# The first feed-forward product by seven products of half the token width, with its weight sums on GpSimd

## The chip, the core and the metric

The kernel runs on one core of a Trainium2 chip. The metric is the device time of one execution in microseconds (us); lower is better. The engines of a core are called as the profile calls them: PE is TensorE (PEld its weight loads), DVE is VectorE, ACT is ScalarE, POOL is GpSimd and SP is SyncE, which only issues transfers here. SBUF is the on-chip memory that all of them read, PSUM holds the sums that PE makes (POOL does not use it here), HBM is the chip's main memory.

## What is computed

An encoder of two layers on 512 tokens of width 1024, all in 32-bit floats. Each layer adds to x the result of two attention groups, and then that of a feed-forward part, with a norm ahead of each; a last norm ends the network. Only the feed-forward part is changed:

```python
h = rmsnorm(x, mlp_norm[l])
u = jnp.square(jax.nn.relu(jnp.einsum('bsd,df->bsf', h, w_ff1[l])))   # 1024 -> 4096: the first product
x = x + jnp.einsum('bsf,fd->bsd', u, w_ff2[l])                        # 4096 -> 1024: the second product
```

## The kernel before, in words

**Numbers in two parts.** PE multiplies a rounded 32-bit format. So that little is lost, each operand is split in two: hi, the rounded value, and lo, the remainder. A product is three matmuls, hi by hi, hi by lo and lo by hi; `three` (L284) issues them. A weight tile is split by two instructions, a copy that rounds on ACT (`round`, L109) and a subtraction raw - hi on DVE (L125). Activations are split the same way by `split` (L232 to L235).

**Weights.** `_unit_list` (L50) writes down all weight units in the order in which PE uses them. `_Weights` loads raw units of 128 x 1024 by SP's queue into a ring of three tiles (`load`, L98), splits them (`do_split`, L132) and hands them out (`next`, L153). While a unit is being used, units up to three behind it may be split: `next` asks for four from the one in use, and there are four places for split tiles in the feed-forward part. Hooks kept in `W.then` start what may follow the split of a unit (L150).

**The feed-forward part** (from L826) works in 4 groups of 1024 of the 4096 inner columns (`GROUPS`, L25). A group has two stages:

- *The first product*, L1012: eight blocks of 128 inner columns. `block` (L297) runs 8 x 3 matmuls with 512 tokens as the moving operand, from a unit of kind "1". `evict_u` (L873) takes the result out of PSUM: relu and square on ACT, and then the seven forms of u that the second product needs, by subtractions on DVE (L889, L892), each split in hi and lo.
- *The second product*, L1022: a product of 2 x 2 by 2 x 2 blocks by the seven-product algorithm (in Winograd's form), so seven block products in place of eight. Their names are in `FORMS` (L41). Each form has two weight units of kind "f" of 12 matmuls of 512 columns each. The sums of weight quarters that the forms need are made by the transfers: a tile is loaded by SP's queue, and another quarter is added in flight by an accumulating transfer that POOL issues (`grow` and `fetch`, L842 to L857). `gather` (L901) adds finished chains to the result y on DVE, with the norm's factor.

Each group's second product follows its first at once; PE works through both in the order of the program. PSUM has 8 banks in four sets: "mm" 2, "s" 3, "o" 1 and "t" 2 (L170). Instructions are queued on each engine in an order that the framework fixes at compile time from the program's order and its own estimates; `behind` adds an order by hand. A queue is worked off in that order: an instruction that waits holds up those behind it.

**x, cos and sin.** x stays in SBUF through the feed-forward part and gets y added at the end of layer 0 (`back`, L923). The cos and sin tables are loaded again for layer 1 in group 1 of layer 0. In layer 1 the same two tiles take the gains of the last norm (L1006), which `weigh` and `store` (L968 to L981) use at the very end. The attention part comes ahead of each feed-forward part; its softmax-like weights are multiplied on POOL (`s1_sb`, L539) and its norm on POOL too (`finish`, L686).

Of the kernel before, what the change touches and what calls it, by code (L numbers as in the profile page):

```python
# [41 lines left out]
SIDE = {"11": 0, "x4": 1, "21": 2, "x3": 3, "x1": 4, "x2": 5, "22": 6}  # L42
HOME = {"11": 0, "x1": 0, "x3": 1, "x2": 1, "x4": 1, "22": 2, "21": 2}
CHAIN = {"11": "X", "x2": "X", "x1": "X", "22": "X", "x3": "V", "x4": "V", "21": "Y"}
# [5 lines left out]
def _unit_list():  # L50
# [5 lines left out]
    for l in range(L):  # L56
# [13 lines left out]
        for g in range(GROUPS):  # L70
            for f in range(2 * GP):
                units.append(("1", l, g * 2 * GP + f))
            for form in FORMS:
                for c in range(GP // 2):
                    units.append(("f", l, g, form, c))
# [6 lines left out]
_RING = [i for i, u in enumerate(_UNITS) if u[0] != "f"]  # L82
_SLOT = {u: n for n, u in enumerate(_RING)}
_QUAD = [(l, g, q, c) for l in range(L) for g in range(GROUPS) for c in range(GP // 2) for q in QUADS]


class _Weights:
    def __init__(self, nc, dram, rawp, splp):
        self.nc, self.dram, self.rawp = nc, dram, rawp
        self.loaded = self.split = self.used = self.turn = 0  # L90
        self.raw, self.tiles, self.home, self.then = {}, {}, {}, {}
        self.depth = 3
        self.eager = False
        self.pools = [splp]
        self.owner = {}
        self.rest_of = {}

    def load(self, n):  # L98
        while self.loaded < min(n, len(_RING)):
# [28 lines left out]
    def spot(self, i):  # L128
        n = 2 * len(self.pools) if _UNITS[i][0] in "1f" else 2
        return self.turn % n if self.turn < n else 0  # L130

    def do_split(self, n, ahead=None):  # L132
        while self.split < min(n, len(_UNITS)):
# [4 lines left out]
            if kind != "f":  # L138
                self.load(_SLOT[i] + 1)
# [8 lines left out]
            if kind != "f":  # L148
# [14 lines left out]
def trunk(ctx, tc, opened, xT, w, w2, gfin, lamv, cos, sin, out):  # L163
# [4 lines left out]
    ps = ctx.enter_context(tc.tile_pool(name="ps", bufs=2, space=PSUM))  # L168

# [18 lines left out]
    ssq = cp.tile([P, S], F32, tag="ssq", name="ssq")  # L188
    rbc = cp.tile([P, S], F32, tag="rbc", name="rbc")
    cos_t = cp.tile([P, S], F32, tag="cos", name="cos_t")  # L190
    sin_t = cp.tile([P, S], F32, tag="sin", name="sin_t")
# [40 lines left out]
    def split(hi, lo, src):  # L232
        a = nc.scalar.activation(hi, src, AF.Copy)  # L233
        nc.vector.tensor_tensor(out=lo, in0=src, in1=hi.bitcast(F32), op=ALU.subtract)  # L234
        return a  # L235
# [87 lines left out]
    for l in range(L):  # L323
# [502 lines left out]
        with ExitStack() as fctx:  # L826
# [9 lines left out]
            kept = [[fp.tile([P, 1024], F32, tag=f"q{k}{c}", name=f"q{k}{c}_{l}0") for c in range(GP // 2)] for k in range(3)]  # L836
            i0 = W.used

            def unit(g, form, c):
                return i0 + g * (2 * GP + len(FORMS) * GP // 2) + 2 * GP + FORMS.index(form) * GP // 2 + c  # L840

            def fetch(g, form, c):  # L842
                k = HOME[form]
                if g:
                    kept[k][c] = fp.tile([P, 1024], F32, tag=f"q{k}{c}", name=f"q{k}{c}_{l}{g}")
                W.raw[unit(g, form, c)] = kept[k][c]
                nc.sync.dma_start(kept[k][c], quad(g, "12" if form == "x3" else form, c))
                if form == "x3":
                    nc.gpsimd.dma_start(kept[k][c], quad(g, "22", c), accum_op=ALU.add)

            def grow(g, form, q, c):
                t = kept[HOME[form]][c]
# [4 lines left out]
                W.raw[unit(g, form, c)] = t  # L857

            for g in range(GROUPS):
                for c in range(GP // 2):  # L860
                    for form, fn, args in (
                            ("11", grow, (g, "x1", "12", c)), ("x3", grow, (g, "x2", "11", c)),
                            ("x2", grow, (g, "x4", "21", c)), ("21", grow, (g, "22", "22", c)),
                            ("x1", fetch, (g + 1, "11", c)), ("x4", fetch, (g + 1, "x3", c)),
                            ("22", fetch, (g + 1, "21", c))):
                        if g + 1 < GROUPS or fn is grow:
                            W.then.setdefault(unit(g, form, c), []).append(lambda fn=fn, args=args: fn(*args))
            for form in ("11", "x3", "21"):
                for c in range(GP // 2):
                    fetch(0, form, c)  # L870
            W.pools.append(f2)

            def evict_u(pt, g, k, forms):  # L873
                pair, which = k // 2, k % 2
                nm = f"{l}{g}{pair}"
                if which == 0:
                    forms[pair] = (
                        fp.tile([P, 8, 256], F32, tag="F", name="F" + nm),
                        fp.tile([P, 7, 256], F32R, tag="Ah", name="Ah" + nm, bufs=GP),
                        fp.tile([P, 7, 256], F32R, tag="Al", name="Al" + nm, bufs=GP))  # L880
                F, hi, lo = forms[pair]
# [3 lines left out]
                if which == 0:  # L885
# [3 lines left out]
                nc.vector.tensor_tensor(  # L889
                    out=F[:, 4:6, :], in0=F[:, 1:3, :], in1=F[:, 0:1, :].to_broadcast([P, 2, 256]), op=ALU.subtract)  # L890
                for o, i, j in ((6, 5, 1), (7, 6, 3)):
                    nc.vector.scalar_tensor_tensor(  # L892
                        out=F[:, o, :], in0=F[:, i, :], scalar=-1.0, in1=F[:, j, :], op0=ALU.mult, op1=ALU.subtract)
                W.forms = split(hi[:, 3:7, :], lo[:, 3:7, :], F[:, 4:8, :])
# [264 lines left out]
```

## Time and profile before

| | |
|---|---|
| median of 3 runs | 1146.6 us (1146.29 to 1146.64) |
| profiled execution | 1146.63 us, of it the span of the trace 1144.7 us |
| granted PE clock | 0.998 |
| instructions | 15843 |
| HBM read, written | 138.18 MB, 2.10 MB |

The profile's page gives for each engine its busy time, its share of the span and its number of instructions. Slices are the span in 40 equal parts, a digit being the busy share in tenths. A row of a group of instructions reads: line, engine, operation, output <- inputs, shapes, xcount | busy us in total, mean ns of one | idle time of the engine just before them, and what ended it. A row of the timeline reads: start (us from the start of the span), duration, engine, line, operation, and in brackets how long the engine had been idle and what released it. A row of the windows gives for one stretch of time its length and for each engine its busy time and number of instructions, then the granted clock, the share of the DMA engines and the rate of transfers. The recorded durations of successive matmuls overlap, as one starts before the last is through.

### The profile page before, as it was taken

How to read it: one execution, taken by the hardware profiler on the slowest of the kernel's cores; microseconds unless marked ns; L12 is line 12 of the kernel's file. 1: busy time of each engine (PE TensorE's matmuls, PEld its weight loads, DVE VectorE, ACT ScalarE, POOL GpSimd, SP SyncE). 2: the span in 40 equal slices, each digit the busy share in tenths (PEclk: the TensorE clock that was granted, in tenths of full speed). 3: DMA queues.
4: the chain of work that ended last, by engine and by line, in shares of the span. 5: the costliest groups of instructions: out<-in, count | busy, mean ns of one | idle time of the engine just before them, and what ended most of it. 6: DMA issues, size and time to landing. Idle time of an engine off the chain costs nothing.

```text
span 1144.7 us, 15843 instructions
## 1 busy us (share of the span) xinstructions
PE 1135.8 (99%) x5749; PEld 967.2 (84%) x5749; DVE 811.4 (71%) x1313; ACT 641.1 (56%) x1147; POOL 141.0 (12%) x225
## 2 busy tenths in 40 slices
PE   9999999999999999999999999999999999999997
PEld 7899889888888888888888998988888888888886
DVE  7898788775645756756778877887657467566576
ACT  6456666556656445455345666665574454553554
POOL 1000333100101101001000013330011011010010
PEclk9999999999999999999999999999999999999999
DMA  7664353257754845836226634522758458358162
GB/s 256 164 187 141 106 167 98 70 205 166 186 176 90 206 154 94 247 119 103 82 74 192 195 111 144 151 72 76 234 115 211 157 92 232 136 93 256 41 126 92
DMA packets 55853, 166.47 MB, mean 145 GB/s; under 512 B 6880, under 2 KB 8160, under 8 KB 55776
## 3 DMA queue, kind: packets, MB, share of 16 engines
q1 hardware_dynamic: 46128, 131.36, 35.3%
q0 software_dynamic: 9216, 33.56, 17.1%
q8 instruction: 45, 0.74, 0.3%
q10 hardware_dynamic: 432, 0.56, 0.1%
q14 instruction: 32, 0.26, 0.1%
HBM read 138.18 MB, written 2.10 MB: 123 GB/s over the span
## 4 chain that ended last, share of the span: by engine, by line
PE 98%; DVE 1%; issue 1%; ACT 0%; POOL 0%; POOLq 0%; DVEq 0%; ACTq 0%
PE f L287 10%; PE f L288 10%; PE f L289 10%; PE X L288 5%; PE X L287 5%; PE X L289 5%; PE wo L287 3%; PE wo L289 3%; PE wo L288 3%; PE V L288 2%; PE V L289 2%; PE V L287 2%; PE Y L289 1%; PE Y L287 1%; PE Y L288 1%; PE T1s L606 1%
## 5 line engine op out<-in xcount | busy, mean ns | idle before, releaser
L125 DVE TENSOR_TENSOR wlo<-raw,whi 128x1024 fp32r<-128x1024 f32 (+1 forms) x130 | 154.3, 1190 | 109.2 <-ACT whi L109 107.1
L109 ACT ACTIVATE whi<-raw 128x1024 fp32r<-128x1024 f32 (+1 forms) x130 | 131.8, 1018 | 142.3 <-PE f L288 44.5
L287 PE MATMUL f<-h_hi,whi 128*128 128x512 f32 x512 | 199.9, 390 | 0.0
L289 PE MATMUL f<-h_hi,wlo 128*128 128x512 f32 x512 | 199.6, 390 | 0.0
L109 ACT ACTIVATE whi<-q 128x512 fp32r<-128x512 f32 x224 | 129.9, 623 | 124.3 <-PE X L289 44.0
L288 PE MATMUL f<-h_lo,whi 128*128 128x512 f32 x512 | 199.5, 390 | 0.0
L125 DVE TENSOR_TENSOR wlo<-q,whi 128x512 fp32r<-128x512 f32 x224 | 145.5, 688 | 73.5 <-ACT whi L109 69.6
L289 PEld LDWEIGHTS f<-h_hi,wlo 128*128 128x128 f32 x512 | 96.2, 188 | 19.9
L287 PEld LDWEIGHTS f<-h_hi,whi 128*128 128x128 f32 x512 | 96.2, 188 | 19.7
L288 PEld LDWEIGHTS f<-h_lo,whi 128*128 128x128 f32 x512 | 96.2, 188 | 19.7
L234 DVE TENSOR_TENSOR Al<-F,Ah 128x256 fp32r<-128x256 f32 (+2 forms) x96 | 74.8, 779 | 46.0 <-ACT Ah L233 46.0
L287 PE MATMUL X<-whi,Ah 128*128 128x512 f32 x248 | 97.0, 391 | 0.0
L289 PE MATMUL X<-whi,Al 128*128 128x512 f32 x248 | 96.7, 390 | 0.0
L288 PE MATMUL X<-wlo,Ah 128*128 128x512 f32 x248 | 96.6, 390 | 0.0
L233 ACT ACTIVATE Ah<-F 128x256 fp32r<-128x256 f32 (+2 forms) x96 | 67.6, 704 | 50.0 <-DVE F L892 48.1
L856 POOL DMA_DIRECT2D q<-in_w x48 | 41.8, 871 | 424.0 <-DVE wlo L125 396.1
L289 PEld LDWEIGHTS X<-whi,Al 128*128 128x128 f32 x248 | 46.6, 188 | 9.7
L287 PEld LDWEIGHTS X<-whi,Ah 128*128 128x128 f32 x248 | 46.6, 188 | 9.5
L288 PEld LDWEIGHTS X<-wlo,Ah 128*128 128x128 f32 x248 | 46.6, 188 | 9.5
L287 PE MATMUL V<-whi,Ah 128*128 128x512 f32 x128 | 49.9, 390 | 0.0
L289 PE MATMUL V<-whi,Al 128*128 128x512 f32 x128 | 49.9, 390 | 0.0
L288 PE MATMUL V<-wlo,Ah 128*128 128x512 f32 x128 | 49.9, 390 | 0.0
(658 smaller groups left out, 2562.2 us busy)
## 6 DMA issues: line engine op xcount, KB each, us to landing
raw<-in_w SPq DMA_DIRECT2D x126, 512.0 KB, 3.5
q<-in_w SPq DMA_DIRECT2D x64, 512.0 KB, 5.5
q<-in_w POOLq DMA_DIRECT2D x64, 512.0 KB, 5.5
x<-in_xT SPq DMA_DIRECT2D x8, 256.0 KB, 4.4
out_xT<-y SPq DMA_DIRECT2D x6, 256.0 KB, 2.1
raw<-in_w SPq DMA_DIRECT2D x6, 128.0 KB, 4.1
cos_t<-in_cos SPq DMA_DIRECT2D x2, 256.0 KB, 4.9
sin_t<-in_sin SPq DMA_DIRECT2D x2, 256.0 KB, 4.0
```

The lines of the kernel that those rows point to most:

```text
L109: return self.nc.scalar.activation(o, src, AF.Copy)
L125: self.last = h, nc.vector.tensor_tensor(out=lo[:, a:b], in0=raw[:, a:b], in1=hi[:, a:b].bitcast(F32), op=ALU.subtract)
L233: a = nc.scalar.activation(hi, src, AF.Copy)
L234: nc.vector.tensor_tensor(out=lo, in0=src, in1=hi.bitcast(F32), op=ALU.subtract)
L287: nc.tensor.matmul(pt, ah, bh, start=first, stop=False, skip_group_check=goes_on)
L288: nc.tensor.matmul(pt, ah, bl, start=False, stop=False, skip_group_check=goes_on)
L289: nc.tensor.matmul(pt, al, bh, start=False, stop=last, skip_group_check=goes_on)
L606: nc.tensor.transpose(pt[:, off : off + P], u["w"][qi][:, kb * P : (kb + 1) * P], ident)
L856: nc.gpsimd.dma_start(t, quad(g, q, c), accum_op=ALU.add)
```

## The change

The first product of seven of the eight half groups of a layer is computed by the seven-product algorithm as well. The half (g, j) = (0, 0) stays as it was, four whole blocks. Each other half, a "quad group", covers 512 inner columns: seven forms, each with one unit of kind "s" of 128 x 1024 (two pairs of 128 columns by four pieces of the inner width 512), used by 2 x 4 x 3 matmuls with 256 tokens as the moving operand.

- **Forms of h.** During the four whole blocks `h_form` makes three forms of h from x with the norm's gain (16 DVE operations of 128x256, and splits), and overwrites a quarter of h with a fourth one.
- **Weight sums.** Four quarters of w_ff1 (roles a, b, c, d) are loaded for each quad group by SP's queue into five tiles: the three of the raw ring, the pair cos/sin and the pair ssq/rbc. Four sums of 128x1024 on POOL make the forms: e = c + b, b + a, a + e, d + a. Each is issued by a hook behind a split of the unit whose tile it overwrites or reads.
- **Evictions.** In a quad group three results are copied from PSUM by ACT, two are added and one is subtracted by DVE, and four differences and sums of 128x512 that make the forms of u run on POOL (`pool_tt`), in place of the subtractions on DVE. The whole blocks use POOL for theirs too, eight of 128x256.
- **x in HBM.** x's tile is the work space of the quad groups. In layer 0 eight stores on SP's queue put x into HBM at the start of the feed-forward part, and eight loads bring it back in the last group's second product. In layer 1, x has been turned into y before.
- **Tables.** cos and sin are loaded behind the last split of layer 0; the final gains are loaded into x's tile in the last group of layer 1.
- **Ring.** Raw units of the next layer are loaded only when the last quad group has been split (`limit`). The order of two forms in `SIDE` is exchanged.

The core of the diff:

```diff
+CHAIN1 = {"11": "X", "x3": "V", "x2": "X", "21": "Y", "x1": "X", "x4": "V", "22": "X"}
...
         for g in range(GROUPS):
-            for f in range(2 * GP):
-                units.append(("1", l, g * 2 * GP + f))
+            for j in range(2):
+                if (g, j) == (0, 0):
+                    units.extend(("1", l, f) for f in range(GP))
+                else:
+                    units.extend(("s", l, g, j, form) for form in FORMS)
...
+            def add(n, to, by, other=None):
+                if n < len(groups):
+                    nc.gpsimd.tensor_tensor(
+                        out=piece(n, to), in0=piece(n, other or to), in1=piece(n, by), op=ALU.add)
+
+            def first_sums(n):
+                add(n, "e", "c", "b")
+                add(n, "b", "a")
...
+            for n, (g, j) in enumerate(groups):
+                then(("s", l, g, j, "11"), add, n, "a", "e")
+                then(("s", l, g, j, "x3"), bring, n + 1, "c")
+                then(("s", l, g, j, "21"), add, n, "d", "a")
+                then(("s", l, g, j, "21"), bring, n + 1, "a")
+                then(("s", l, g, j, "x1"), bring, n + 1, "b")
...
+                then(("s", l, g, j, "22"), first_sums, n + 1)
...
+            if not last:
+                park = dp.tile([KC, P, S], F32, tag="park", name="park")
+                for c in range(KC):
+                    nc.sync.dma_start(park[c], x[:, c, :])
...
+            def scaled(out, c0, half, other, op):
+                for c in range(4):
                     nc.vector.scalar_tensor_tensor(
+                        out=out[:, c, :], in0=x[:, c0 + c, half], scalar=gcol("mlp", l, c0 + c), in1=other[:, c, :],
+                        op0=ALU.mult, op1=op)
...
+            def quad_group(g, j):
+                X, V = bank("mm", f"X{l}{g}{j}"), bank("s", f"V{l}{g}{j}")
+                Y = bank("o" if j else "s", f"Y{l}{g}{j}")
...
+                for n, form in enumerate(FORMS):
+                    u = W.next("s")
...
+                    for pr in range(2):
+                        for c in range(4):
+                            at = 512 * pr + P * c
+                            three(to[ch][:, 256 * pr : 256 * pr + 256], (u[0][:, at : at + P], u[1][:, at : at + P]),
+                                  (h[0][:, c, :], h[1][:, c, :]),
+                                  form in ("11", "x3", "21") and pr == c == 0, pr == 1 and c == 3, True)
+                    if form == "11":
+                        nc.scalar.copy(m11, X)
+                    elif form == "x3":
+                        nc.scalar.copy(v3, V)
+                    elif form == "x2":
+                        nc.scalar.copy(sx, X)
+                    elif form == "21":
+                        nc.vector.tensor_tensor(out=F[1], in0=Y, in1=m11, op=ALU.add)
+                        nc.scalar.activation(F[1], F[1], AF.Relu)
+                        nc.scalar.activation(F[1], F[1], AF.Square)
+                        split(hi[0], lo[0], F[1])
+                    elif form == "x1":
+                        nc.vector.scalar_tensor_tensor(
+                            out=F[2], in0=X, scalar=-1.0, in1=v3, op0=ALU.mult, op1=ALU.subtract)
+                    elif form == "x4":
+                        nc.vector.tensor_tensor(out=F[0], in0=V, in1=sx, op=ALU.add)
+                        nc.scalar.activation(both, both, AF.Relu)
+                        nc.scalar.activation(both, both, AF.Square)
+                        split(hi[1], lo[1], F[2])
+                        pool_tt(F[1], F[1], F[0], ALU.subtract)
+                        pool_tt(F[0], F[2], F[0], ALU.subtract)
+                        pool_tt(F[2], F[2], F[1], ALU.add)
...
+                        split_less(hi[5], lo[5], F[2])
+                    else:
+                        nc.scalar.activation(F[3], X, AF.Relu, scale=-1.0)
+                        nc.scalar.activation(F[3], F[3], AF.Square)
+                        split(hi[2], lo[2], F[3])
+                        pool_tt(F[3], F[2], F[3], ALU.subtract)
+                        W.forms = split(hi[6], lo[6], F[3])
```

243 lines of the change are left out of this document (167 added, 76 removed).

## The prediction, made before the changed kernel ran

> **What bounds the kernel now.** I read the page first: busy shares, the slices, the chain that ended last.
>
> ```profile
> PE 1135.8 (99%) x5749; PEld 967.2 (84%) x5749; DVE 811.4 (71%) x1313; ACT 641.1 (56%) x1147; POOL 141.0 (12%) x225
> ...
> PEclk9999999999999999999999999999999999999999
> ...
> PE 98%; DVE 1%; issue 1%; ACT 0%; POOL 0%; POOLq 0%; DVEq 0%; ACTq 0%
> ```
>
> PE does not idle, its clock is full, and 98% of the chain is PE. A gain can come only from fewer or shorter matmuls, and it lasts as long as what feeds PE keeps up. So the next view is the busy time by stage, here for one group of layer 0: first product, then second.
>
> ```profile
> core 0: us, PE busy (x) PEld busy (x) DVE busy (x) ACT busy (x) POOL busy (x), PEclk, DMA share, GB/s
> 323.00:366.00 43.00, 43.00 (x192) 35.63 (x191) 21.27 (x30) 23.80 (x37) 2.62 (x3) 1.00 0.40 104
> ...
> 447.00:485.00 38.00, 38.00 (x170) 31.48 (x169) 28.47 (x42) 18.35 (x29) 4.40 (x5) 1.00 0.80 198
> ```
>
> In the first product DVE is busy 21 of 43 us, in the second 28.5 of 38, and POOL almost never. The change puts work on both.
>
> **What PE gains.** A matmul's recorded length overlaps the next, so the price is the distance between starts. Two rounds of weights that each wait for a block of 24 matmuls of 512 columns, and a run of 256-wide matmuls:
>
> ```profile
> 333.30 1.06 ACT L109 ACTIVATE whi<-raw 128x1024 fp32r<-128x1024 f32 x1 [2.78 <-PE f L288]
> ...
> 344.18 1.06 ACT L109 ACTIVATE whi<-raw 128x1024 fp32r<-128x1024 f32 x1 [2.32 <-PE f L288]
> ```
>
> ```profile
> 583.69 0.28 PE L428 MATMUL p1w<-mdl,h_hi 128*128 128x256 f32 x1
> ...
> 586.09 0.28 PE L428 MATMUL p1w<-mdl,h_hi 128*128 128x256 f32 x1
> ```
>
> The first pair is two blocks apart: 10.88 us, 5.44 a block, 226.7 ns a matmul. The second is 20 matmuls apart: 2.40 us, 120 ns each. Per layer, 28 of the 32 blocks become 7 quad groups. Four blocks are 96 matmuls of 512, 21.76 us; a quad group is 7 forms of 24 matmuls of 256, 168 x 120 ns = 20.16 us. PE saves 1.60 us a quad group, 14 x 1.60 = **22.4 us** in all: half-width matmuls cost more than half, so of the eighth of the arithmetic little is left.
>
> The Trainium skill speaks for more: "TensorE: Matmul & The Clock Gate", "Back-to-back issue gap", gives a warm gap of N/2.4 plus 2.5 ns, 215.8 and 109.2 ns here. By that a quad group would save 20.7 - 18.3 = 2.4 us and the kernel 33 us. The rows, 226.7 and 120, disagree with it and decide.
>
> **What the other engines get.** Rows by form, and the second product's DMA issues on POOL:
>
> ```profile
> L125 DVE TENSOR_TENSOR wlo<-raw,whi 128x1024 fp32r<-128x1024 f32 x122 | 151.3, 1242 | 109.2 <-ACT whi L109 107.1 <-DMA q<-in_w 1.5 <-ACT lam_ex L315 0.3
> ...
> L109 ACT ACTIVATE whi<-raw 128x1024 fp32r<-128x1024 f32 x122 | 128.9, 1059 | 142.3 <-PE f L288 44.5 <-DMA raw<-in_w 24.5 <-PE V L289 20.9
> ...
> L856 POOL DMA_DIRECT2D q<-in_w x48 | 41.8, 871 | 424.0 <-DVE wlo L125 396.1 <-DMA q<-in_w 27.9
> L909 DVE SCALAR_TENSOR_TENSOR y<-X,r,y 128x512 f32<-128x512 f32 x58 | 41.7, 749 | 4.9 <-PE X L289 3.8
> L884 ACT ACTIVATE F<-F 128x512 f32<-128x512 f32 x64 | 40.3, 630 | 1.4
> L234 DVE TENSOR_TENSOR Al<-F,Ah 128x1024 fp32r<-128x1024 f32 x32 | 39.2, 1224 | 28.1 <-ACT Ah L233 28.1
> L883 ACT ACTIVATE F<-f 128x512 f32<-128x512 f32 x64 | 37.5, 587 | 12.9 <-DVE Al L234 8.0 <-PE f L289 4.9
> ...
> L892 DVE SCALAR_TENSOR_TENSOR F<-F 128x256 f32<-128x256 f32 x64 | 27.0, 422 | 1.1
> ...
> L889 DVE TENSOR_TENSOR F<-F 128x512 f32<-128x512 f32 x32 | 22.1, 689 | 6.5 <-ACT F L884 6.5
> ```
>
> *ACT, per quad group*: 7 weight rounds x 1.06 = 7.4; three copies out of PSUM x 0.59 = 1.8; relu, square and rounds at 0.63 for 512, 1.06 for 1024: F1 1.9, F0 with F2 4.4, F3 2.5. Together **18.0 us** in 20.2. It fits, without room.
>
> *DVE, per quad group*: 7 weight remainders x 1.24 = 8.7; one 1024-wide remainder 1.22; four of 512 at 0.69 and one scalar_tensor_tensor at 0.75 = 3.5; three operations that read PSUM, two at 0.69 and one at 0.75 = 2.1. **15.5 us**. The four blocks that it replaces cost 10.6 (half of 21.27): seven weight units stand where four stood.
>
> *POOL, per quad group*: four sums of 128x1024 and four of 128x512. No row shows a 1024-wide sum. The nearest are these; the first is by itself:
>
> ```profile
> 149.28 1.29 POOL L686 TENSOR_TENSOR os<-os,rb 128x512 f32<-128x512 f32 x1
> ```
>
> ```profile
> 143.05 1.09 POOL L539 TENSOR_TENSOR sig0s<-sig0s,C0s 128x512 f32<-128x512 f32 x1 [0.67 <-DVE C0s L536]
> ```
>
> ```profile
> 148.53 0.63 POOL L539 TENSOR_TENSOR sig0s<-sig0s,C0s 128x256 f32<-128x256 f32 x1 [1.63 <-DVE C0s L536]
> ```
>
> From 256 to 512 L539 grows by 0.46, so 1024 would take 1.09 + 0.92 = 2.0 us; scaled by L686, 1.29 x 2.0/1.09 = 2.37. I take 1.29 and 2.37, as the new sums read whole aligned tiles like os and rb: 4 x 2.37 + 4 x 1.29 = **14.6 us** (low end 12.4).
>
> **The point that decides: DVE and POOL get in each other's way.**
>
> ```profile
> 143.50 1.73 DVE L125 TENSOR_TENSOR wlo<-raw,whi 128x1024 fp32r<-128x1024 f32 x1
> ```
>
> ```profile
> 148.69 0.56 DVE L234 TENSOR_TENSOR xl<-T0s,xh 128x384 fp32r<-128x384 f32 x1 [0.31 <-ACT xh L233]
> ```
>
> ```profile
> 118.94 1.23 DVE L125 TENSOR_TENSOR wlo<-raw,whi 128x1024 fp32r<-128x1024 f32 x1 [0.38 <-ACT whi L109]
> ```
>
> ```profile
> 119.82 1.50 POOL L686 TENSOR_TENSOR os<-os,rb 128x512 f32<-128x512 f32 x1 [1.33 <-ACT rb L282]
> ```
>
> The remainder that starts at 143.50 falls into the POOL product of 143.05 to 144.14 and takes 1.73 us instead of 1.24: it waited until about 0.15 us before POOL's end. The other way round, the POOL product of 119.82 met a remainder that ran to 120.17 and took 1.50 instead of 1.29. At 148.69 a DVE operation with one operand in PSUM ran beside the POOL product of 148.53 in 0.56 us, unharmed. So a DVE operation with both operands in SBUF and a POOL product take turns. All remainders of weights are of that sort, 13.4 of DVE's 15.5 us, and so are all POOL sums.
>
> The Trainium skill states this as an exclusive lock ("SBUF — State Buffer", "Who interferes with whom"): the loser waits for the whole instruction. The trace agrees, to 0.15 us. By that rule alone, with nothing else late, each sum would block DVE for its whole length.
>
> **The sum.** I add DVE and POOL as one resource over a group, since the second product's 38 us let a backlog drain. Before, a group takes PE 8 x 5.44 + 14 x 2.72 = 81.6 us. After, PE needs 2 x 20.16 + 38.1 = 78.4. DVE and POOL need 28.5 (second product, row above) + 2 x 15.5 + 2 x 14.6 = **88.7 us**. So the pair is the bound, 7.1 us over the old time. Two corrections, that DVE's PSUM readers and the ends of a POOL sum can overlap, and that the chain round, remainder, sum, round leaves gaps, have opposite signs; I leave both out.
>
> The first group of a layer has one quad group. Its four whole blocks carry on DVE 5.0 of weights (4 x 1.24), 5.3 of evictions (two pairs, each 0.42 + 0.69 + 0.69 + 0.42 + 0.42), and the forms of h: 16 operations of 256 at 0.42 = 6.7 and four remainders at 1.24 = 5.0. That is 22.0 + 15.5 + 28.5 = 66.0 on DVE; POOL has 14.6 and eight differences of 256 x 0.63 = 5.0. Sum 85.6, 4.0 over.
>
> Six full groups and two first ones: 6 x 7.1 + 2 x 4.0 = **50.6 us longer**.
>
> *Moved at no cost, and their cover:* x goes to HBM in 8 stores (layer 0 only) and comes back in 8 loads on SP's queue; behind the stores stand the first loads of weight pieces. At the 198 GB/s of the quoted window 2.1 MB takes 10.6 us, covered by the units already split (four, 21.8 us); without cover, up to 10 us once. The loads run during the last second product, 38 us. The added waits on POOL: a sum waits for a weight remainder, and behind it in POOL's queue stand the second product's accumulating DMAs (0.87 us each), whose data the following weight rounds await. The final gains load later, in the last group, under its forms; by this row, up to 5 us if uncovered.
>
> ```profile
> cos_t<-in_cos SPq DMA_DIRECT2D x2, 256.0 KB, 4.9
> ```
>
> The profiled execution lasted 1146.6 us with a span of 1144.7, its 1.9 us outside kept; it is the median of the runs too. 1146.6 + 50.6 = **1197 us**.
>
> **Rivals.**
>
> *A. Everything hides*: PE stays the bound, 1146.6 - 22.4 = 1124 us. For it: ACT's 18.0 and DVE's 15.5 each fit in 20.2, and four units are split ahead. Against it: 15.5 + 14.6 = 30.1. It needs POOL to work beside DVE's PSUM readers and idle time only. Price per group at most -3.2 us; it decides from where DVE and POOL overlap by over 10.3 us a group (88.7 to 78.4). With 7.1 of them they break even. This is the faster side. 0.17.
>
> *B. Half overlaps*: with the low POOL price (12.4) and 0.3 us of each of the 16 sums free, a group needs 28.5 + 31 + 24.8 - 4.8 = 79.5, beside 81.6 before; gaps between waits bring it near the old time or above: 1140 to 1170. 0.20, a little of it faster or within the bound.
>
> *C. The backlog does not drain in the second product*, since splits run only four units ahead and POOL's queue is in order: each quad group takes its own 30.1 instead of 21.8. 14 x 8.3 = 116, 1263 us. For it: the sums for x3, x2, x4 form a chain round, remainder, sum. Against it: the second product's DVE has 9.6 us of room. 0.13.
>
> *D. The edit does not do what it says*: the 256-wide matmuls run slower than 120 ns because stationary weights change with every one. Each of the 5749 matmuls has its weight load in the quoted profile too, those of the run among them, so 0.02; at 130 ns it adds 14 x 1.68 = 24 us to PE alone.
>
> Forecast (1170 to 1235): 0.48.
>
> **How the numbers follow.** The range takes in B, and C's lower half: 1138 to 1250, which leaves out most of A and the top of C. Changes under 0.2%, 2.3 us, are about what a measurement of this kernel cannot tell from none. Faster: A and a little of B, 0.18. Within: 0.04. Slower: 0.78.
>
> **What would show it.** Right: in first-product windows PE busy falls below nine tenths; the remainders of weights (L125's group) have a mean over 1.24 us, 1.5 or more; POOL sums of 1024 show 2.0 us or more; the chain has DVE and POOL shares of several per cent. Wrong: PE stays at 99%, with L125 at 1.24. C is told from the forecast by second-product windows that stay at 38 us while every quad group takes 28 or more; D by start distances over 120 ns with no idle time before.

## The result, and the profile after

The changed kernel takes **1239.5 us** (median of 4 runs, 1237.6 to 1240.1); the kernel before takes 1146.6 us on the same chip. The ratio is 1.081, with a 95% interval of 1.079 to 1.083: **92.9 us longer**. The forecast was 1197, in a range up to 1250. So the sign and the mechanism have to be looked at apart from the size.

The page of the changed kernel: busy shares, granted clock, and the chain that ended last.

```profile
PE 1157.1 (93%) x6757; PEld 1017.6 (82%) x6757; DVE 973.4 (79%) x1349; ACT 706.4 (57%) x1227; POOL 408.9 (33%) x353
...
PEclk9999999989998998999999999999899999999999
...
PE 56%; DVE 18%; POOL 8%; issue 6%; ACT 6%; DMA 6%; POOLq 0%; DVEq 0%; SPq 0%; ACTq 0%
```

PE was 98% of the chain and is 56%. DVE and POOL together hold 26%, though DVE is busy only 79% of the span: no engine is full, and yet PE waits. The clock has dips that the kernel before didn't have.

The windows of a full group of layer 1: its two quad groups, then its second product.

```profile
958.20:1008.10 49.90, 44.23 (x337) 43.42 (x336) 40.26 (x32) 28.72 (x40) 27.46 (x13) 0.93 0.32 91
1008.10:1049.60 41.50, 39.62 (x171) 31.37 (x170) 31.89 (x44) 20.68 (x33) 13.76 (x11) 1.00 0.82 196
```

The group takes 91.4 us and took 81.6. A quad group takes 25.0 where four blocks took 21.8, and the second product 41.5 where it took 38.1. In the first row DVE and POOL add up to 67.7 us in 49.9: part of the recorded time of each is waiting for the other. The first groups of the two layers went from 82.1 to 101.4 and from 85.7 to 103.9 us, by the starts of their matmuls.

Groups of instructions, by form:

```profile
L951 POOL TENSOR_TENSOR x<-x 128x512 f32<-128x512 f32 x56 | 93.0, 1661 | 58.1 <-DVE Al L243 30.1 <-ACT x L1035 23.7 <-PE V L304 2.5
...
L132 DVE TENSOR_TENSOR wlo<-T,whi 128x1024 fp32r<-128x1024 f32 x56 | 93.1, 1663 | 34.8 <-ACT whi L116 34.7
...
L243 DVE TENSOR_TENSOR Al<-x,Ah 128x512 fp32r<-128x512 f32 x56 | 67.2, 1201 | 29.1 <-ACT Ah L242 29.1
...
L890 POOL TENSOR_TENSOR T<-T,T 128x1024 f32<-128x1024 f32 x20 | 55.1, 2755 | 15.9 <-DVE wlo L132 14.9
...
L1033 DVE TENSOR_TENSOR x<-V,x 128x512 f32<-128x512 f32 x14 | 9.5, 681 | 0.0
```

Weight remainders of the tiles T take 1663 ns, where the kernel before had 1242, and the remainders of u (L243) 1201 in place of 689, while L1033, which has one operand in PSUM, stayed at 681. The single instructions show how. The timeline of DVE:

```profile
962.22 2.10 DVE L132 TENSOR_TENSOR wlo<-T,whi 128x1024 fp32r<-128x1024 f32 x1 [1.53 <-ACT whi L116]
...
969.88 0.69 DVE L1025 TENSOR_TENSOR x<-Y,x 128x512 f32<-128x512 f32 x1 [0.69 <-PE Y L304]
...
972.71 2.88 DVE L243 TENSOR_TENSOR Al<-x,Ah 128x512 fp32r<-128x512 f32 x1
```

And the timeline of POOL over the same time:

```profile
960.82 2.41 POOL L890 TENSOR_TENSOR waves<-waves,T 128x1024 f32<-128x1024 f32 x1 [5.81 <-DVE wlo L132]
...
969.28 2.41 POOL L890 TENSOR_TENSOR norms<-T,T 128x1024 f32<-128x1024 f32 x1 [6.04 <-DVE wlo L132]
971.76 3.27 POOL L890 TENSOR_TENSOR T<-T,T 128x1024 f32<-128x1024 f32 x1
```

The remainder of 962.22 starts inside the sum of 960.82, which ends at 963.23, and ends 1.09 us after it: a whole remainder after the sum. The remainder of 512 at 972.71 needs 0.69 and takes 2.88, behind the sum of 971.76. DVE's operation of 969.88, with one operand in PSUM, runs inside the sum of 969.28 at its usual 0.69.

What PE waited for, in total us, times and the longest:

```profile
PE X L302 <- ACT x L1019: 16.0, 7, 2.4
PE X L302 <- ACT x L1023: 12.4, 6, 3.0
PE xT L1082 <- ACT y L1083: 11.3, 2, 9.4
```

PE waits at the copies of finished results out of PSUM. ACT makes these copies, but ACT itself stands behind operations that wait for DVE or POOL. The chain at the start of the second product shows the other new wait:

```profile
1009.33 1.34 POOL x L951
1010.74 1.64 POOL x L951
...
1016.51 0.84 POOL x L951
1017.35 0.70 issue
1018.05 5.70 DMA q<-in_w
1023.78 0.64 ACT whi L116
1024.44 0.70 DVE wlo L132
1025.19 0.50 PE X L303
```

POOL issues the accumulating transfer only when the differences ahead of it in its queue are done; the transfer needs 5.7 us, and the second product's weights are late by it.

### The profile page after: what moved, and what is told of

It reads as the page before. It is cut to its first block, busy times and chain, and to the rows that moved or that the text cites. A ratio compares the mean times of both kernels' runs of the same rounds, so it can differ in the third digit from the quotient of the medians.

```text
span 1237.6 us, 18281 instructions
## 1 busy us (share of the span) xinstructions
PE 1157.1 (93%) x6757; PEld 1017.6 (82%) x6757; DVE 973.4 (79%) x1349; ACT 706.4 (57%) x1227; POOL 408.9 (33%) x353
## 3 DMA queue, kind: packets, MB, share of 16 engines
q0 software_dynamic: 9216, 33.56, 15.5%
## 4 chain that ended last, share of the span: by engine, by line
PE 56%; DVE 18%; POOL 8%; issue 6%; ACT 6%; DMA 6%; POOLq 0%; DVEq 0%; SPq 0%; ACTq 0%
DVE wlo L132 8%; POOL x L951 5%; DVE Al L243 4%; PE X L303 4%; PE X L304 4%; PE X L302 4%; DMA q<-in_w 4%; ACT whi L116 2%; PE Y L302 2%; PE Y L303 2%; PE Y L304 2%; PE V L303 1%; PE V L302 1%; PE V L304 1%; PE wo L302 1%
## 5 line engine op out<-in xcount | busy, mean ns | idle before, releaser
L243 DVE TENSOR_TENSOR Al<-x,Ah 128x512 fp32r<-128x512 f32 (+1 forms) x70 | 96.5, 1379 | 38.8 <-ACT Ah L242 38.8
L132 DVE TENSOR_TENSOR wlo<-T,whi 128x1024 fp32r<-128x1024 f32 x56 | 93.1, 1663 | 34.8 <-ACT whi L116 34.7
L951 POOL TENSOR_TENSOR x<-x 128x512 f32<-128x512 f32 x56 | 93.0, 1661 | 58.1 <-DVE Al L243 30.1
L116 ACT ACTIVATE whi<-raw 128x1024 fp32r<-128x1024 f32 (+1 forms) x74 | 72.6, 987 | 44.7 <-issue 20.3
L132 DVE TENSOR_TENSOR wlo<-raw,whi 128x1024 fp32r<-128x1024 f32 (+1 forms) x74 | 85.9, 1164 | 13.3 <-ACT whi L116 12.9
L302 PE MATMUL X<-hxh,whi 128*128 128x256 f32 x224 | 70.4, 314 | 24.3 <-ACT x L1019 16.0
L242 ACT ACTIVATE Ah<-x 128x512 fp32r<-128x512 f32 (+1 forms) x70 | 49.8, 712 | 50.3 <-POOL x L951 49.9
L302 PE MATMUL X<-h_hi,whi 128*128 128x256 f32 x224 | 66.6, 297 | 12.5 <-ACT x L1023 12.4
L132 DVE TENSOR_TENSOR wlo<-waves,whi 128x512 fp32r<-128x512 f32 (+1 forms) x60 | 57.1, 972 | 22.4 <-ACT whi L116 22.2
L303 PE MATMUL X<-hxl,whi 128*128 128x256 f32 x224 | 68.5, 306 | 0.0
L304 PE MATMUL X<-hxh,wlo 128*128 128x256 f32 x224 | 68.4, 306 | 0.0
L304 PE MATMUL X<-h_hi,wlo 128*128 128x256 f32 x224 | 66.2, 295 | 0.7 <-DVE wlo L132 0.7
```

The costliest lines, as they stand in the source:

```text
L116: return self.nc.scalar.activation(o, src, AF.Copy)
L132: self.last = h, nc.vector.tensor_tensor(out=lo[:, a:b], in0=raw[:, a:b], in1=hi[:, a:b].bitcast(F32), op=ALU.subtract)
L302: nc.tensor.matmul(pt, ah, bh, start=first, stop=False, skip_group_check=goes_on)
L303: nc.tensor.matmul(pt, ah, bl, start=False, stop=False, skip_group_check=goes_on)
L304: nc.tensor.matmul(pt, al, bh, start=False, stop=last, skip_group_check=goes_on)
L951: return nc.gpsimd.tensor_tensor(out=out, in0=a, in1=b, op=op)
```

## The experiments

**Theory**: DVE operations with two operands in SBUF and POOL operations that read SBUF take turns; the sums and differences cost their turns. **Rivals**: POOL's queue alone (what matters is how long POOL is occupied, so that transfers and differences behind the sums are late); the chains of rounds and sums, whichever engine runs them; and DVE's own load. Ratios and intervals belong to runs with several rounds; the others are single runs, beside 1146.5 us of the kernel before.

### One part taken away or moved

**The weight sums left out** (the form x3 takes the quarter c in place of the sum e):

```diff
             def add(n, to, by, other=None):
-                if n < len(groups):
-                    nc.gpsimd.tensor_tensor(...)
+                pass
```

> Leaves out the four 128x1024 sums of weights on POOL in every quad group (the seven forms use raw quarters of the weights, so this part of the computation is changed); the differences of 128x512 on POOL stay. Theory (DVE and POOL take turns, so their work adds up): a group needs 28.5 + 31.0 + 8 x 1.28 = 69.7 us of DVE and POOL, less than PE's 78.4, so PE is the bound again in steady groups, about 80 us a group where 91.4 was measured: 1130 to 1160 us. Rival 1 (seven weight units and the longer chain of evictions are too much for ACT and DVE by themselves): nearly nothing changes, 1210 or more. Rival 2 (no port, the sums are only long and POOL's queue is in order): same as the theory here.

Measured: 1166.2 us, 6 us above the theory's range; rival 1 (1210 or more) fell. Quad groups 41.75 us a pair, second products 40.8. Of the 92.9 us, 73.3 go with the sums. This run doesn't tell the theory from rival 2, which expected the same; the runs with memsets below do.

**The differences on DVE** (`pool_tt`), **the sums on DVE** (`add`), and **both**:

```diff
-                return nc.gpsimd.tensor_tensor(out=out, in0=a, in1=b, op=op)
+                return nc.vector.tensor_tensor(out=out, in0=a, in1=b, op=op)
```

> The differences of 128x512 (and 128x256) that make the forms of u go back to DVE; the weight sums stay on POOL. Theory: 28.5 + 31.0 + 8 x 0.69 of DVE and 8 x 2.36 of POOL are 83.9 us a group, 4.8 below the 88.7 of the prediction's sum, so some 4 to 6 us a group less than the 91.4 measured: 1190 to 1215 us. Rival 1 (DVE's own load): slower than 1240, as DVE gets 5.5 us a group more. Rival 2 (POOL's queue alone): POOL has 9.4 us of 20 a quad group, DVE 18.3, both fit, so 1130 to 1150.

> The four weight sums of a quad group go to DVE (1.23 us each by the 128x1024 remainder); the differences stay on POOL. Theory: 28.5 + 31.0 + 8 x 1.23 of DVE and 8 x 1.28 of POOL are 79.6 us a group, about PE's 78.4, and with the gaps of the first measurement (2.7) 82: 1160 to 1185 us. Rival 1 (DVE's own load): slower than 1240. Rival 2 (POOL's queue alone): 1130 to 1150.

> Weight sums and differences all on DVE, no tensor work on POOL in the feed-forward part. Theory: DVE needs 28.5 + 31.0 + 8 x 1.23 + 8 x 0.69 = 74.9 us a group, under PE's 78.4, though each quad group alone has 23.2 of DVE against 20.2 of PE, so stalls of 1 to 3 us a group are left: 1130 to 1160 us. Rival 1 (DVE's own load is what stalls PE): the slowest of the four, above 1260, as DVE gets 7.7 us more a quad group. Rival 2 (POOL's queue alone): like the theory, 1130 to 1160, with the delay of the second product's accumulating transfers gone as well.

Measured: 1200.2 with the differences moved, 1204.9 with the sums moved, 1167.2 with both (ratio 1.018, 1.016 to 1.020). The differences cost DVE 0.69 us each and took POOL 1.28 or more, so moving them frees more turns than it loads on DVE: the theory's range held, and the rival of POOL's queue alone (1130 to 1150) fell. With the sums moved the theory's range (1160 to 1185) was missed by 20 us, and the rivals' too: the quad groups still took 44.3 to 45.9 us a pair. The expectation had added the work over a whole group, 79.6 us, where it seems to fit; a quad group alone has 25.5 us of it in turn beside PE's 20.2, and the second products got longer as well. With both moved the range (1130 to 1160) was missed by 7 us; the rival of DVE's own load (above 1260) fell.

The work that goes in turn, worked out from the prediction's rows (DVE's 15.5 us, a difference 1.29 on POOL or 0.69 on DVE, a sum 2.37 on POOL or 1.22 on DVE, four of each), orders the quad groups of these runs, beside the 20.2 us that PE needs (pairs of the six full groups, halved). In the runs with the sums on DVE most of the measured pairs have 5 to 7 matmuls of the second product among theirs, 1.1 to 1.6 us a pair. The work in turn doesn't order the whole times: with the sums moved the second products of the full groups, those matmuls included, take 42 to 44 us, with the differences moved 39.0 to 39.8 (but for layer 0's last, where x comes back).

| run | in turn, us per quad group | measured, us per quad group |
|---|---|---|
| the changed kernel | 30.1 | 23.7 to 25.4 |
| differences on DVE | 27.7 | 22.2 to 24.4 |
| sums on DVE | 25.5 | 22.2 to 23.0 |
| both on DVE | 23.1 | 20.4 to 23.0 |
| no sums, differences on POOL | 20.7 | 20.9 |
| no sums, differences on DVE | 18.3 | 20.15 |

Where the work in turn is well over PE's time, the quad group is longer, by up to about half of what is over (up to all of it where DVE alone has the work); the rest overlaps or is put off. The gains of the two moves, 39 and 35 us, add up to nearly the gain of both, 72 us: it isn't one of the two loads on POOL alone that decides.

**No sums, and the differences on DVE**: the change with POOL out of the way.

> Leaves out the weight sums as the first experiment did (raw quarters in their place), and the differences run on DVE: no tensor work on POOL in the feed-forward part, 18.3 us of DVE a quad group. What is still open is why leaving out the sums alone gave 1166 and not 1124, the prediction's time with everything hidden. Theory (what is left there is the differences on POOL that take turns with the remainders): 1126 to 1145 us. Rival (ACT's 18.0 us of 20.2 and the length of the eviction chain stall PE whatever POOL does): within 10 us of 1166. The all-on-DVE version (1167) then splits into the price of the sums on DVE and the rest.

Measured: 1139.0 us, ratio 0.993 (0.991 to 0.994), within the theory's range. The windows of one second product and one pair of quad groups:

```profile
931.80:970.90 39.10, 38.73 (x171) 31.52 (x170) 31.57 (x47) 20.04 (x33) 4.80 (x6) 1.00 0.82 198
970.90:1011.20 40.30, 40.30 (x338) 40.30 (x337) 29.22 (x36) 28.74 (x40) 2.16 (x3) 1.00 0.46 121
```

Now PE fills the quad groups: 40.3 us a pair, 20.15 each, the figure that the prediction worked out of the 120 ns. So ACT's 18.0 us and the longer chain of weight units fit, and PE gets its 1.6 us a quad group. But with sums that cost nothing the kernel gains only 7.6 us: seven quad groups a layer save 21 us, the second products, 38.1 before, take 39.1 to 40.2 (44.1 in the last group of layer 0, where x comes back from HBM; 39.5 before), 13 us in all. Why they take longer, apart from x's return, was not worked out.

### Reading or only occupying

This is the test that tells turns on a port from time on a queue. **The kernel before, with useless POOL work beside it**: at each unit of the first product one sum of 128x1024 that reads two tiles, or two memsets of that size that only write.

```diff
+                if kind == "1" and self.zeros2:
...
+                    self.nc.gpsimd.tensor_tensor(
+                        out=self.zeros2[0], in0=self.zeros2[0], in1=self.zeros2[1], op=ALU.add)
```

> The kernel before with one useless 128x1024 sum on POOL (both operands in SBUF, result unused) started beside each first-product weight remainder, by a one-column operation that waits for the same round; some 57 such sums. Nothing of the computation is changed. Theory (a shared port, turns): the remainders of these units lengthen from 1.24 by up to the sum's 2.0 us, or the sums from 2.35 by 1.1; per pair about 3.4 us in all. Rival (no port; what lengthened in the changed kernel is something else): remainders stay at 1.24 and sums at 2.35. The time: within 10 us of before in both cases, as the stage has 20 us of DVE to spare.

> The same with two memsets of 128x1024 on POOL in place of the sum: about as long on POOL (estimated 2 us, from 0.42 us for 384 columns and 0.20 for 128 on the page of before), but reading nothing. Theory (the remainder's second operand is read through what POOL reads through): remainders stay at 1.24, time as before. Rival (any POOL work beside it slows DVE): remainders lengthen as with the sums.

Measured: 1171.3 with the sums, 1157.2 with the memsets; 10.8 us in each of the two come from the extra tiles alone, as two runs below show. Remainders of weights, and POOL's work, with sums:

```profile
L126 DVE TENSOR_TENSOR wlo<-raw,whi 128x1024 fp32r<-128x1024 f32 x122 | 185.9, 1526 | 63.7 <-ACT whi L110 62.6 <-DMA q<-in_w 0.7 <-ACT lam_ex L322 0.3
...
L147 POOL TENSOR_TENSOR zero<-zero,zero 128x1024 f32<-128x1024 f32 x62 | 166.8, 2691 | 4.9
```

And with memsets:

```profile
L126 DVE TENSOR_TENSOR wlo<-raw,whi 128x1024 fp32r<-128x1024 f32 x122 | 151.3, 1242 | 112.9 <-ACT whi L110 109.7 <-DMA q<-in_w 1.5 <-DMA raw<-in_w 1.3
...
L148 POOL MEMSET zero<- 128x1024 f32 x124 | 121.0, 1005 | 5.8
```

In the run with reading sums the remainder takes 1526 ns in the mean, with memsets 1242, the same as in the kernel before. The mean hides the meetings: with the sums 88 of the 122 remainders keep their 1.2 us and 34 take 1.4 to 3.4; with the memsets 6 take 1.4 to 1.8, as many as before. The Trainium skill ("SBUF — State Buffer", "Who interferes with whom") has it so: a DVE instruction with two SBUF inputs contends with a GpSimd instruction that reads SBUF, not with one that only writes it. These rows agree. The times, expected within 10 us of before, were missed in both runs.

**The changed kernel with writing in place of summing**: each sum became three memsets on the same tile at the same place in the queue.

```diff
-                    nc.gpsimd.tensor_tensor(
-                        out=piece(n, to), in0=piece(n, other or to), in1=piece(n, by), op=ALU.add)
+                    for wd in (1024, 1024, 512):
+                        nc.gpsimd.memset(piece(n, to)[:, 0:wd], 0.0)
```

> The changed kernel with each of GpSimd's weight sums replaced by three memsets of 1024, 1024 and 512 columns on the sum's own tile, at the sum's place: about 2.5 us of GpSimd as before, on the same queue with the same waits, but it reads nothing. (The summed weights are zero in it, so this part of the computation is changed.) Theory (a GpSimd operation that reads takes turns with VectorE's two-operand operations, one that only writes does not): nearly all that leaving the sums out gave, 1165 to 1185, quad groups 42 to 44 us per pair. Rival (what hurts is how long the sums keep GpSimd and its queue, so that the differences and the transfers behind them are late): the time of the changed kernel, 1225 to 1245, quad groups 49 to 50 us per pair.

Measured: 1174.0 us, within the theory's range, quad groups 41.75 us a pair. Rows of this run:

```profile
L132 DVE TENSOR_TENSOR wlo<-T,whi 128x1024 fp32r<-128x1024 f32 x56 | 75.7, 1351 | 41.4 <-ACT whi L116 41.4
L891 POOL MEMSET T<- 128x1024 f32 x68 | 64.0, 953 | 79.5 <-DMA T<-in_w 51.8 <-DVE wlo L132 25.8 <-issue 0.5
```

POOL is busy 379 us here, nearly the 409 of the changed kernel, and 65.5 us of the loss are gone. The remainders take 1351 ns, as in the run without sums (1348), where the differences are on POOL too. The rival of the queue's time is left with 7.8 us (1174.0 less 1166.2). One thing more differs: a memset doesn't wait for the sum's other operand, and what that gave was not measured apart.

So the 92.9 us come in steps, each a difference of two runs:

| step | us |
|---|---|
| PE's gain, less the second products' loss (no sums, differences on DVE) | -7.6 |
| differences on POOL in place of DVE | +27.2 |
| POOL occupied for the length of the sums, reading nothing | +7.8 |
| the sums read SBUF | +65.5 |

The price of the differences depends on the order: with the sums still on POOL, moving them gave 39.3. No run had them only write, so how much of it is turns and how much is time on POOL's queue is not shown.

### Sums made by transfers

**All four sums by accumulating transfers, the differences on DVE**, as the kernel before does for the second product; a tile is loaded, and one to three quarters are added in turn:

```diff
+            def more(n, role, q):
...
+                    nc.gpsimd.dma_start(piece(n, role), w1[_FIRST.index((l, *groups[n], q))], accum_op=ALU.add)
```

> The weight sums are made in flight by accumulating transfers that POOL only issues (four loads and four accumulations a quad group, as the second product has them), the differences run on DVE, and form 21 comes ahead of x2 so that an accumulation has two units of time. Nothing is left out. Theory (only work on DVE and POOL's port stalls PE): like the run without sums, 1126 to 1150, faster than before or level with it. Rival (the transfers are the next bound: by the page of before the software queue takes 17.1% of the span for 64 accumulations, 3.1 us each, and the hardware queue about 1.5 us a load of 512 KB, so 18.4 us in a quad group of 20.2, and one accumulation is 6 us behind the split that it waits for): 1165 or more, with PE waiting for rounds that wait for DMA.

Measured: 1271.7 us, ratio 1.109 (1.107 to 1.111), worse than the change. The theory behind it was wrong, and its rival (the transfers are the next bound, 1165 or more) held. PE's longest wait:

```profile
PE V L303 <- ACT whi L117: 49.5, 14, 5.4
```

The transfers of this run, KB each and us from issue to landing:

```profile
T<-in_w POOLq DMA_DIRECT2D x56, 512.0 KB, 7.4
```

Once in each of the 14 quad groups PE waits for a form whose tile is added to late: an addition can only be issued when the form before it has been split, and lands 7.4 us after. That is 49.5 of the 132.7 us that this run takes over the one without sums; the rest lies in shorter waits and a slower clock (0.954) and was not worked out.

**Two sums by transfers issued long ahead into tiles that change places, two on DVE**, with the differences on DVE too:

```diff
+                then(("s", l, g, j, "x2"), more, n + 1, "e", "22")
...
+                then(("s", l, g, j, "x4"), more, n + 1, "b", "11")
```

> Nothing of the computation is left out. Two of the four weight sums of a unit, 12+22 and 12+11, are made by accumulating transfers that are issued most of a unit set ahead into tiles that change places, and the other two by VectorE, which makes the differences of x too; GpSimd makes none. Theory (GpSimd's sums and VectorE's remainders take turns on the memory, and a transfer is late only when its chain has no slack): VectorE has 15.5 + 2 x 1.4 + 2.45 = 20.7 us of work per quad group against 20.16 us of TensorE, so about 41.5 us per pair of quad groups and 39.5 for the second product: 81 x 6 + first groups near those of the version with all sums on VectorE, 1140 to 1160 in all. Rival (transfers that accumulate cost as much wherever they stand, since each of them keeps the port or the software queue busy): half of what the version with all four by transfers lost, quad groups at 48 to 52 us per pair, 1190 to 1225.

Measured: 1175.3 us (1164.9 to 1178.2), ratio 1.026 (1.025 to 1.028). Both ranges were missed. One second product and one pair of quad groups, from an execution of 1164.9 us:

```profile
378.90:420.40 41.50, 38.95 (x170) 31.38 (x170) 32.77 (x48) 20.11 (x33) 5.08 (x6) 1.00 0.94 219
420.40:460.70 40.30, 40.30 (x338) 40.30 (x337) 32.60 (x39) 29.15 (x40) 4.79 (x7) 1.00 0.65 170
```

The chain at the start of that second product:

```profile
378.56 12.38 DMA q<-in_w
391.03 0.64 ACT whi L116
```

The quad groups are at PE's 40.3 with all four sums made: that part of the expectation held. The loss moved into the second products, 39.4 to 43.8 us, where the DMA engines are now 94% busy and one accumulating transfer took 12.4 us, and into the first groups. No version that computes everything beats the kernel before; with free sums there would be 7.6 us to win, and every way tried to make the sums costs more.

### The extra tiles alone

The two runs with useless POOL work had their 512-wide matmuls some 230 ns apart, without waits. **The kernel before with their extra tiles only**, then **with the tile of one column made 32 wide**, so that the tiles behind it begin at multiples of 128 bytes again:

```diff
-            W.tick = fp.tile([P, 1], F32, tag="tick", name=f"tick{l}")
+            W.tick = fp.tile([P, 32], F32, tag="tick", name=f"tick{l}")
```

> The kernel before with only the extra tiles of the two runs that gave it useless GpSimd work (one of a single column, two of 1024 columns, set once per layer); the work itself is left out. Both of those runs showed the 512-wide matmuls of the feed-forward part some 230 ns apart instead of 226.7, with no waits. If the places of the tiles make this: the first product's group again at 44.2 us and the second's at 38.7, 1155 to 1159. If GpSimd's work beside it makes it: 43.5 and 38.1, 1146 to 1148.

> As the kernel before with the extra tiles only, but the tile of one column (4 bytes a partition) has 32 columns (128 bytes). If the odd offset of the tiles behind it made the wider distance of the 512-wide matmuls: the distances go back to 226.7 ns, 43.5 us for a first product and 38.1 for a second, 1146 to 1148. If other things of the extra tiles made it (the amount of memory taken, or which addresses the weights get): still 44.2 and 38.7, 1156 to 1159.

Measured: 1157.3 and 1157.5 us. Windows of a first and a second product with the extra tiles only:

```profile
323.90:368.10 44.20, 44.20 (x194) 36.06 (x193) 21.27 (x30) 24.47 (x38) 2.62 (x3) 1.00 0.41 104
368.10:406.70 38.60, 38.60 (x169) 31.51 (x168) 29.09 (x43) 18.30 (x29) 4.38 (x5) 1.00 0.81 209
```

PE is busy throughout, its clock is full, and the stages take 44.2 and 38.6 us in place of 43.5 and 38.1. So the tiles alone cost 10.8 us, the odd offset isn't the reason, and the comparison of sums and memsets has to be made against 1157.3: the memsets cost nothing, the sums 14.0 us. All of the 14.0 us lie in two stages of the first groups: layer 0's second product (45.3 us for 38.8 with the tiles alone) and layer 1's first product (55.7 for 48.1). In the other six groups the stages last 44.2 and 38.7 us with the sums as without them. There DVE has room: it is busy 21 of the 44 us of such a first product (first row above). Why the distances grow stays open. The changed kernel isn't touched by it: there the 512-wide matmuls of the feed-forward part are 227 ns apart in the median.

## Why the prediction was right, and where it was off

- **PE's saving, 1.60 us a quad group: right.** 20.15 us where POOL is out of the way. That each half-width matmul costs 120 ns (rival D at 0.02) is so too, while the clock is full.
- **The point that decides, taking turns: right**, and for the sums now shown: the loss follows whether POOL reads, not whether it is busy. The signs named for it came: PE is busy 44.2 of 49.9 us in the quad groups, the remainders of the tiles T take 1663 ns, and DVE and POOL have 18% and 8% of the chain. For the differences (27.2 us or more) turns are the likely cause, not a shown one.
- **The price of a sum, 2.37 us, and of a difference, 1.29: right** for one that meets nobody. The shortest in the trace took 2.35 and 1.28. The recorded means (2755 and 1661 ns in the rows above) hold waiting.
- **The sum of DVE and POOL for a full group, 88.7 us: a little small.** Measured are 91.4 to 92.2, and 88.5 and 89.6 in the last group of a layer, which has no next quad group to prepare; the six are 53.7 us longer than before, in place of 42.6. That is 11 of the 42 us that the forecast was short. What the prediction left out on the side of loss was larger than the overlap of PSUM readers: the gaps, and the clock, for which it has no term (0.93 in the window of the two quad groups above).
- **The first groups, +4.0 each: the step that failed most.** Measured +19.3 and +18.2. A sum over 85 us evens out what meets at one place. The four whole blocks of layer 0 still take 22.3 us; the quad group behind them takes 32.6, at a clock of 0.84:

```profile
264.40:297.00 32.60, 24.85 (x169) 23.74 (x168) 24.07 (x23) 17.34 (x27) 23.46 (x12) 0.84 0.58 164
```

The sums for it begin only as the whole blocks end, and there they meet the remainders of the forms of h and of the first weights. The first sum, and the last of five DVE operations that follow each other without a gap from 263.05 on:

```profile
262.77 7.44 POOL L890 TENSOR_TENSOR norms<-T,T 128x1024 f32<-128x1024 f32 x1 [2.13 <-PE f L304]
...
266.79 1.22 DVE L243 TENSOR_TENSOR h_lo<-q,h_hi 128x1024 fp32r<-128x1024 f32 x1
```

The sum takes 7.44 us in place of 2.37 and ends 2.2 us after that row of DVE operations, one sum's length: in effect it waited for all five. In layer 1 the same sum takes 6.34 us, and the longest wait of PE, the third in the list of waits above, is a copy on ACT behind a round that waits for a later sum:

```profile
888.72 1.06 ACT L116 ACTIVATE whi<-T 128x1024 fp32r<-128x1024 f32 x1 [5.37 <-POOL T L890]
...
890.80 2.12 PE L1082 MATMUL xT<-edge,x 128*128 128x128 f32 x8 [9.44 <-ACT y L1083]
```

In the run with memsets the first groups took 92.0 and 93.4, with POOL out of the way 83.5 and 85.3. So 19.8 of their 37.5 us go with the reading and 16.6 with the rest of POOL's work. They are 29.5 of the 42 us (19.3 + 18.2 - 8.0).

- **The backlog that drains in the second product: half wrong.** Rival C had 30.1 us for a quad group and 38.1 for a second product; the forecast let the 9.6 us of room in the second product absorb the rest. Measured are 25.0 and 41.4. The quad groups lost less than by C, probably since the splits of four units run ahead. The second product, in place of absorbing, got longer, since its accumulating transfers stand behind POOL's differences: the chain shows 5.7 us of transfer behind differences of 0.84 to 1.64 us, and with the differences on DVE the second products of the full groups take 39.0 to 39.8 (but for layer 0's last), though the sums are still on POOL. The prediction had named that queue, and given it no price.
- **Moves at no cost: nearly.** x's return costs at most 4.6 us (44.1 for 39.5 in the run with POOL out of the way).
- **Rival A's price was out of reach.** It had 1124 us for the case that everything hides. With no sums and the differences on DVE the kernel came to 1139.0, so about 15 us were lost beside any turns with POOL, 13 of them in second products.

The time lay within the range because the misses have one sign and its upper end had been taken from C, not because the size was understood: the measured excess of 92.9 us is 1.8 times the forecast's 50.6.

## What to carry to other kernels

Count DVE's operations with two SBUF operands and POOL's operations that read SBUF as one engine, and make that sum for each stretch in which the results are needed, not over a whole group. An engine that is 12% busy isn't free capacity if its work takes turns with one that is 71% busy; moving the same work onto DVE itself, where it takes half as long, was the better choice of the two. Before believing in a small loss, move the tiles alone.

## What the runs showed of the hardware that was not expected

**PE's clock is halved for 3.4 us or more after a stretch of 3.4 us in which PE was busy less than about half.** Windows of the changed kernel, each 3.4 to 3.6 us:

```profile
984.00:987.60 3.60, 1.34 (x11) 1.14 (x10) 3.03 (x3) 2.28 (x4) 3.60 (x2) 1.00 0.00 0
987.60:991.00 3.40, 3.40 (x17) 3.40 (x17) 1.57 (x2) 0.97 (x3) 2.67 (x2) 0.50 0.50 145
991.00:994.40 3.40, 3.40 (x31) 3.40 (x30) 3.23 (x3) 2.54 (x5) 1.29 (x1) 1.00 0.02 10
994.40:997.80 3.40, 1.52 (x13) 1.32 (x12) 3.40 (x5) 3.38 (x5) 0.00 (x0) 1.00 0.56 151
997.80:1001.20 3.40, 3.40 (x18) 3.40 (x17) 3.40 (x3) 1.90 (x3) 2.53 (x1) 0.50 0.51 163
```

PE is busy 1.34 of 3.60 us, and in the next window it is busy all the time at a clock of 0.50, with 17 matmuls where 31 go at full clock; then again. The longest stalls in the two were 2.3 and 1.9 us. The Trainium skill ("TensorE: Matmul & The Clock Gate", "Part 1: The HAM clock gate (the "warmup" mystery)") has the fall to half rate after at least one idle window of some 3.4 us. The length of the slow pieces agrees; but here a window that was 40% busy was enough. Each slow piece that the trace records before PE's last matmul lasts 3.4 us or a multiple of it. With the trace cut into stretches of that length, 15 stretches of the changed kernel that ran at full clock were busy 0.49 or less, and the clock was halved right behind each; behind none that was busy 0.62 or more was it. The nearest two are 315.17 to 318.58 (busy 1.66 of 3.41 us, then clock 0.50) and 564.34 to 567.75 (2.13 of 3.41, then 1.00). In the variants of the changed kernel those of 0.46 to 0.55 went either way. The way back asks for more: with all sums by transfers, stretches at half clock that were busy 0.62 to 0.80 were followed by another one, and the lowest that brought full clock back, over all variants, was busy 0.80.

Over the whole kernel 231 half-width matmuls start some 213 ns apart in place of 120, 21.9 us in all; with POOL out of the way three do. How much of the 21.9 us would have gone into waiting anyway was not settled.

**An accumulating transfer of 512 KB landed after 5.5 to 8.1 us in the median, by the kernel.** It is 5.5 us in the kernel before, the same as for a load into the same tiles; 6.2 in the changed kernel, beside 4.9 for such a load and 3.6 to 5.2 for others of this size; 7.4 and 7.6 with all four sums made so; 7.1 and 8.1 with two, where one transfer held up the chain for 12.4 us. And **extra tiles alone** widened the distance of 512-wide matmuls by 1.5% without a wait.
